# A hybrid attention and RG-LRU layer on one core: modulation quads of four-k groups in pairs, a seventh raw slot, and the rotary tables moved

## The chip, the cores and the metric

The kernel runs on one core of a Trainium2 chip. The metric is the device time of one execution in microseconds (us), a median of runs. The core has five engines that run apart from each other and wait on semaphores: TensorE (PE, with its weight loads shown as PEld), VectorE (DVE), ScalarE (ACT), GpSimd (POOL, which here only issues DMAs) and SyncE (SP, which issues nearly all loads). Line numbers such as L521 are lines of the kernel before, unless the text says "of the changed kernel"; the changed kernel's lines stand up to 8 higher.

## The reference

One layer with x and ctx of 256 tokens by 4096 columns each. What it computes, cut to what matters here:

```python
mod = silu(c) @ w_ada + b_ada                       # shift, scale, gate; also with c_ctx
h_x = rmsnorm(x, norm_w) * (1 + scale_x) + shift_x  # and h_c from ctx
q, k, v, ga, xl, gl = split(h @ w_in)               # 4096 x 9216; for ctx k, v and xl are used
q, k = rope(rmsnorm(q)), rope(rmsnorm(k))           # per head of 128; latent tokens only
att = softmax(q k^T) v                              # keys and values of x and ctx
lru = two scans over short_conv(xl), with gates from block-diagonal weights
mix = concat(rmsnorm(att) * silu(ga), rmsnorm(lru) * silu(gl))
out = x + gate_x * (mix @ w_out)
```

All arithmetic is float32; the large products are made of rounded high and low parts, three matmuls each.

## The kernel before

Every weight comes in pieces of 512 KB into one of six "raw" slots. SP issues these loads in the order of the tasks that use them, and the next one as soon as a slot is free. A planner (`Plan.order`) writes out one fixed order of tasks with its own costs; each engine then runs its part of that order, first come first served.

**Projection stage** (to about 665 us). The 4096 rows of `w_in` are walked in groups of k tiles of 128 rows: groups of 1, 1, 2, 2 and 2 k tiles, then six groups of four ("four-k groups"). In a group each weight piece ("unit") is cast to its high part by ACT (L684) and to its low part by DVE (L688), and PE multiplies it in threes (L785 to L787) into a PSUM bank `pm`; DVE adds the bank to the sums `a` in SBUF (L805), which frees it. There are four `pm` banks. A four-k group has 288 such matmuls.

Beside that, the shift and scale of the next group are made from `w_ada` (`mod_tasks`). A "quad" is four k tiles of `w_ada`, 512 columns wide in a four-k group, and so two loads. The shift half's eight quads run on PE (`on_tensor`, L521): four matmuls of 32 output rows side by side in the array, where the matmuls of L785 use all 128. The scale half runs on DVE (L511, two multiply-adds for each k tile, sums in `xin` and `u`); in the first two four-k groups PE has a part of it too. PE folds DVE's sums in at the end (L534). `RUN` says how many quads one PE task takes: `RUN = {1: 2, 2: 1, 4: 1}` by k tiles in the group, so one quad with two loads in a four-k group. The planner may put any other ready PE task between two such tasks.

**Keys and rotary tables.** `rope_tasks` makes, once for k and once for q, a table of cosines and sines times the norm weights. Its first task clears one column of a `wg` slot on DVE (L465) and then has POOL issue two loads (L466, L467, into `wg` and `u`); its second task multiplies them on DVE (L471, L475) into the tile `rope`. `rotate` (L1002 to L1007) uses `rope` and a scratch tile `td` in SBUF.

**After the projection** come q in four chunks with attention and the 16 LRU blocks beside it (L971 to L973 are the matmuls by weights), then the two gates, and from about 1400 us on the output projection, where `scaled` (L1486, L1487) multiplies by the gate through `td` and adds x. The gate third of `w_ada` is summed on DVE (L906) all along from about 630 us.

Of the kernel before, what the change touches and what calls it, by code (L numbers as in the profile page):

```python
# [14 lines left out]
D = 4096  # L15
# [13 lines left out]
NB = 16  # L29
EPS = 1e-6  # L30
C_Q, C_K, C_V, C_GA, C_XL, C_GL = 0, 2048, 2560, 3072, 5120, 7168
RAW = 6
HL = 3
TP = 2
LAT = dict(P=0.2, A=0.14, D=0.14, S=0.15)
# [9 lines left out]
LRU_CHUNKS = 10.2  # L45
MOD_V = {3: (0, 2), 4: (0, 3), 5: (0, 5), 6: (0, 7)}
MOD_V_REST = (0, 8)
RUN = {1: 2, 2: 1, 4: 1}
SWITCH = 0.40
FIRST = (1, 1, 2, 2, 2)  # L50
MOD_LEAD = 0.34
# [23 lines left out]
def dve(n, k=1):  # L75
    return k * (0.07 + n / 962)
# [142 lines left out]
def kernel(  # L219
# [31 lines left out]
    ctx.enter_context(tc.manual_schedule())  # L251


    SLOTS = dict(h4=(22, 1024), a8=(6, 2048), raw=(RAW, 1024), hi=(HL, 1024), lo=(HL, 1024), tp=(TP, 512), ta=(1, 512), td=(1, 512), wg=(2, 514),
                 xin=(1, 512), u=(1, 512), ga=(1, 512), ab=(2, 16), cf=(1, 16), mx=(3, 2), ss=(5, 16), pm=(4, 512), pe=(2, 512), pt=(1, 512), po=(1, 512))
    ROUNDED = ("h4", "hi", "lo")
    free, owner, keepers = {}, {}, []
# [34 lines left out]
        return slot(cl, [128, 512])  # L292


    plan = Plan({cl: n for cl, (n, _) in SLOTS.items() if cl not in ("raw", "td", "ss", "cf")} | dict(lh=1, ah=3, lg=1), RAW)
    add = plan.add

    def play(tasks):
# [33 lines left out]
    nc.sync.dma_start(cin[:, 1, :], c_ctx.rearrange("(p k) -> p k", p=128))  # L332
    sc32 = [slot("wg", [128, 16 * KT + 2]) for _ in range(2)]
    sc = cp.tile([128, 2, KT], F32, name="sc")
    tnh = slot("td", [128, 2, KT])
    for i in range(2):
        V.memset(sc32[i], 0.0)
    V.memset(epsc, EPS)
# [22 lines left out]
    kwc = parT[:, 1, 112:113]  # L361
    hba, hbx, lam = parT[:, 2, 0:32], parT[:, 2, 32:64], parT[:, 2, 64:96]
    lp = cp.tile([128, 2, 32], F32, name="lp")
    rope = cp.tile([128, 2, 2, 128], F32, name="rope")
    gT = cp.tile([128, KT], F32, name="gT")
    st = cp.tile([128, 4, NG], F32, name="st")
    rs = cp.tile([128, 4], F32, name="rs")
# [87 lines left out]
            a = add(fn, [op], [a], pos + step * i, nb=pos - 2 if i == 0 else None, acq=["tp"] if i == 0 else [], rel=["tp"] if fn is finish else [])  # L455
        return a

    def rope_tasks(w, pos, after):

        d = {}  # L460

        def load():
            d["tab"], d["w"] = slot("u", [128, 2, 2, 128]), slot("wg", [128, 128])

            V.memset(d["w"][:, 0:1], 0.0)  # L465
            Q.dma_start(d["w"], w.to_broadcast([128, 128]))  # L466
            Q.dma_start(d["tab"].rearrange("p t f d -> p (t f d)"), consts[:, 130:642])  # L467

        def mul():
            tab, w_ = d["tab"], d["w"]  # L470
            V.tensor_tensor(out=rope[:, :, 0], in0=tab[:, :, 0], in1=w_.unsqueeze(1).to_broadcast([128, 2, 128]), op=ALU.mult)  # L471
            wv = w_.rearrange("p (a h f) -> p a h f", a=2, h=2)
            for t in range(2):
                for h in range(2):
                    V.tensor_tensor(  # L475
                        out=rope[:, t, 1].rearrange("p (a h f) -> p a h f", a=2, h=2)[:, :, h],
                        in0=tab[:, t, 1].rearrange("p (a h f) -> p a h f", a=2, h=2)[:, :, h], in1=wv[:, :, 1 - h], op=ALU.mult,
                    )
            drop(d["tab"], d["w"])

        a = add(load, [("S", 1.0, 6.0)], after, pos - 12, nb=pos - 14, acq=["u", "wg"])
        return add(mul, [("D", dve(256) + dve(64, 4))], [a], pos, rel=["u", "wg"])


    def mod_tasks(k0, nk, out_, p0, p1, nb, cl, on_v=(0, 0)):
# [394 lines left out]
        else:  # L880
            group_pieces(gi, (0, 1), True)

    k_rope = rope_tasks(k_norm_w, starts[-2] + 16, [p_turned])
    decayed = decay_tasks(starts[-2] + 16, 3.0, p_turned)


# [107 lines left out]
    def rotate(a, t):

        o = slot("td", [128, 4, 128])
        av = a.rearrange("p n (a h f) -> p n a h f", a=2, h=2)
        ov = o.rearrange("p n (a h f) -> p n a h f", a=2, h=2)
        sv = rope[:, t, 1].rearrange("p (a h f) -> p a h f", a=2, h=2)
        for ax in range(2):  # L1000
            for h in range(2):
                V.tensor_tensor(  # L1002
                    out=ov[:, :, ax, h], in0=av[:, :, ax, 1 - h],
                    in1=sv[:, ax, h].unsqueeze(1).to_broadcast([128, 4, 32]), op=ALU.mult,
                )
        V.tensor_tensor(out=a, in0=a, in1=rope[:, t, 0].unsqueeze(1).to_broadcast([128, 4, 128]), op=ALU.mult)
        V.tensor_tensor(out=a, in0=a, in1=o, op=ALU.add)  # L1007
        drop(o)

    ROTATE = dve(128, 4) + dve(512, 2)  # L1010
    res = {}
# [1 line left out]
    def key_tasks(pos):  # L1013
        d = {"ss": slot("ss", [128, 4, 4])}

        def kv(t):
            return accs["k"][:, t].rearrange("p (n d) -> p n d", n=4)

        def mul(t):
            V.tensor_tensor(out=kv(t), in0=kv(t), in1=d["ss"][:, t].unsqueeze(2).to_broadcast([128, 4, 128]), op=ALU.mult)  # L1020

        def turn(t):
            d["pt", t] = bank()
            for n in range(4):
                T.transpose(d["pt", t][:, 128 * n : 128 * n + 128], kv(t)[:, n], ident)

        def put(t):
            if t == 0:
                res["kT"] = a8t([128, 4, 512])
            dst = res["kT"][:, :, 128 * t : 128 * t + 128]  # L1030
            src = d["pt", t].rearrange("p (n k) -> p n k", n=4)
            if t < 2:
                S.copy(dst, src)
            else:
                S.activation(dst, src, AF.Copy, scale=kwc)
            drop(d["pt", t])
            if t == 3:
                drop(accs["k"])

        sq = [add(lambda t=t: sum_squares(kv(t), d["ss"][:, t]), [("A", SUMSQ)], [acc_last["k"]], pos + 2 * t, acq=["ta"], rel=["ta"]) for t in range(4)]  # L1040
        nrm = add(lambda: norm_cols(d["ss"]), [("A", ROOT, "root"), ("D", 0.17)], sq, pos + 8)
        prev, rots = None, []
        for t in range(4):
            p = pos + 10 + 5 * t
            a = add(lambda t=t: mul(t), [("D", dve(512))], [nrm], p)
            if t < 2:
                a = add(lambda t=t: rotate(kv(t), t), [("D", ROTATE)], [a, k_rope], p + 1)
                rots.append(a)
# [8 lines left out]
    def q_head_tasks(j, ps, ends, pos, after):  # L1057
        d = {"ss": slot("ss", [128, 4, 4])}

        def pv(t):  # L1060
            return ps[t].rearrange("p (n d) -> p n d", n=4)

        def mul(t):
            a = d["aa", t] = slot("tp", [128, 4, 128])
            for n in range(4):
                S.activation(a[:, n], pv(t)[:, n], AF.Copy, scale=d["ss"][:, t, n : n + 1])
            drop(ps[t])

# [395 lines left out]
    for j in range(8):  # L1464
# [89 lines left out]
```

## Time and profile before

| | |
|---|---|
| median of 3 runs | 1770.1 us (1766.76 to 1772.22) |
| profiled execution | 1768.89 us, span 1767.1 us, mean granted PE clock 0.995 |
| PE busy | 1712.0 us, 97% of the span |
| DVE busy | 1390.0 us, 79% |
| ACT busy | 854.4 us, 48% |
| raw loads | 800 of 512 KB, 255 GB/s of all DMA over the span |

The span is the time from the first to the last instruction on the core; 1.8 us of the execution lie outside it. [...] A busy engine is not always an engine at its peak: where PE has queued work without a gap, only the distance between starts tells its pace.

### The profile page before, as it was taken

The page shows a single profiled execution, that of the slowest core. Times are in us where ns is not written, and L with a number is a line of the kernel's source. Part 1 is how long each engine was busy: PE and PEld are TensorE (multiplying, and loading weights), DVE is VectorE, ACT ScalarE, POOL GpSimd, SP SyncE. Part 2 cuts the span into 40 slices and gives each one's busy share as a digit, 9 for nine tenths or more (in the row PEclk, how much of TensorE's full clock was granted, in tenths as well). Part 3 has the DMA queues.
Part 4 walks back from the last instruction along what each step waited for, and adds up shares of the span by engine and source line. Part 5 has one row for each costly group of instructions (what it writes and reads, how often), then busy time and mean ns, then how long its engine had stood idle before and what let it go on. Part 6 is the DMA issues. An engine that isn't in the chain of part 4 may idle for free.

```text
span 1767.1 us, 22676 instructions
## 1 busy us (share of the span) xinstructions
PE 1712.0 (97%) x8189; PEld 1310.1 (74%) x8189; DVE 1390.0 (79%) x2001; ACT 854.4 (48%) x1254; POOL 58.3 (3%) x93
## 2 busy tenths in 40 slices
PE   4999999999999998999999999999999999999998
PEld 2455667676776677877777778888788788888887
DVE  2368879798989887566799779989987988686864
ACT  5422232232423233357876867777677543333332
POOL 0000000000000000000000000000000000000000
PEclk9999999999999999999999999999999999999999
DMA  9999988988797874854467548777876799898983
GB/s 326 332 343 328 325 310 258 324 269 309 232 326 259 285 251 135 275 172 132 146 206 231 158 119 274 222 240 216 266 253 191 224 335 335 277 334 270 336 275 113
DMA packets 252976, 451.22 MB, mean 255 GB/s; under 512 B 14848, under 2 KB 56432, under 8 KB 252352
## 3 DMA queue, kind: packets, MB, share of 16 engines
q1 hardware_dynamic: 246624, 428.43, 74.0%
q0 software_dynamic: 6240, 21.35, 3.5%
q8 instruction: 64, 1.05, 0.2%
q14 instruction: 48, 0.39, 0.1%
HBM read 441.33 MB, written 8.39 MB: 254 GB/s over the span
## 4 chain that ended last, share of the span: by engine, by line
PE 66%; DVE 17%; DMA 9%; issue 4%; ACT 4%; SPq 1%; DVEq 0%; POOL 0%; ACTq 0%; POOLq 0%
PE pm L971 13%; PE pm L973 13%; PE pm L972 13%; DMA raw<-in_w_ada_dram 7%; PE pm L785 6%; PE pm L786 6%; PE pm L787 6%; DVE lo L688 5%; DVE u L511 2%; PE po L521 2%; PE pt L521 2%; DVE xin L511 2%; ACT hi L684 2%; DVE ga L906 1%; DVE a L805 1%
## 5 line engine op out<-in xcount | busy, mean ns | idle before, releaser
L684 ACT CAST hi<-raw 128x1024 fp32r<-128x1024 f32 x416 | 435.9, 1049 | 714.9 <-PE pm L973 288.4
L688 DVE TENSOR_TENSOR lo<-raw,hi 128x1024 fp32r<-128x1024 f32 x416 | 505.9, 1220 | 178.2 <-ACT hi L684 176.2
L971 PE MATMUL pm<-hi,h 128*128 128x512 f32 x1280 | 514.4, 402 | 0.0
L972 PE MATMUL pm<-lo,h 128*128 128x512 f32 x1280 | 498.9, 390 | 3.9 <-DVE lo L688 3.8
L973 PE MATMUL pm<-hi,h 128*128 128x512 f32 x1280 | 499.1, 390 | 0.0
L785 PE MATMUL pm<-hi,h 128*128 128x512 f32 x768 | 315.7, 411 | 8.7 <-DVE a L805 7.1
L786 PE MATMUL pm<-lo,h 128*128 128x512 f32 x768 | 302.2, 393 | 0.8 <-DVE lo L688 0.8
L787 PE MATMUL pm<-hi,h 128*128 128x512 f32 x768 | 301.9, 393 | 0.0
L972 PEld LDWEIGHTS pm<-lo,h 128*128 128x128 f32 x1280 | 240.7, 188 | 57.6 <-DVE lo L688 5.6
L971 PEld LDWEIGHTS pm<-hi,h 128*128 128x128 f32 x1280 | 240.5, 188 | 51.7 <-issue 4.8
L973 PEld LDWEIGHTS pm<-hi,h 128*128 128x128 f32 x1280 | 240.2, 188 | 50.9
L785 PEld LDWEIGHTS pm<-hi,h 128*128 128x128 f32 x768 | 145.4, 189 | 97.5 <-issue 47.4
L906 DVE SCALAR_TENSOR_TENSOR ga<-raw,sc,ga 128x512 f32<-128x512 f32 x248 | 185.9, 749 | 7.6 <-DMA raw<-in_w_ada_dram 2.4
L787 PEld LDWEIGHTS pm<-hi,h 128*128 128x128 f32 x768 | 145.6, 190 | 32.1
L786 PEld LDWEIGHTS pm<-lo,h 128*128 128x128 f32 x768 | 145.8, 190 | 27.5 <-DVE lo L688 1.3
L511 DVE SCALAR_TENSOR_TENSOR xin<-raw,sc,xin 128x512 f32<-128x512 f32 (+1 forms) x188 | 135.3, 720 | 31.2 <-DMA raw<-in_w_ada_dram 31.1
L805 DVE TENSOR_TENSOR a<-pm,a 128x512 f32<-128x512 f32 x202 | 132.4, 683 | 32.7 <-PE pm L787 32.3
L511 DVE SCALAR_TENSOR_TENSOR u<-raw,sc,u 128x512 f32<-128x512 f32 (+1 forms) x188 | 135.3, 720 | 0.0
L521 PE MATMUL po<-raw,wg 128*32 128x256 f32 (+2 forms) x560 | 61.7, 474 | 27.2 <-DMA raw<-in_w_ada_dram 27.0
L521 PEld LDWEIGHTS po<-raw,wg 128*32 128x32 f32 x560 | 14.7, 119 | 55.8 <-DMA raw<-in_w_ada_dram 26.1
L645 ACT ACTIVATE ta<-pe,ab 128x256 f32<-128x256 f32 x64 | 36.0, 563 | 38.9 <-PE pe L635 31.3
L521 PE MATMUL pt<-raw,wg 128*32 128x512 f32 (+2 forms) x456 | 48.0, 474 | 4.9 <-DMA raw<-in_w_ada_dram 4.8
(189 smaller groups left out, 1299.8 us busy)
## 6 DMA issues: line engine op xcount, KB each, us to landing
raw<-in_w_ada_dram SPq DMA_DIRECT2D x384, 512.0 KB, 5.6
raw<-in_w_in_dram SPq DMA_DIRECT2D x288, 512.0 KB, 4.7
raw<-in_w_out_dram SPq DMA_DIRECT2D x128, 512.0 KB, 5.0
h<-in_x_dram SPq DMA_DIRECT2D x8, 512.0 KB, 7.7
h<-in_ctx_dram SPq DMA_DIRECT2D x8, 512.0 KB, 10.8
xl_d<-a POOLq DMA_DIRECT2D x4, 1024.0 KB, 6.8
xin<-xl_d POOLq DMA_DIRECT2D x16, 256.0 KB, 4.5
a<-in_x_dram POOLq DMA_DIRECT2D x8, 512.0 KB, 7.0
```

Source lines behind the costliest of these rows:

```text
L511: V.scalar_tensor_tensor(out=a, in0=d["w"][:, i], scalar=s_, in1=a, op0=ALU.mult, op1=ALU.add)
L521: T.matmul(d["ps"][32 * q : 32 * q + 32, :], sc32[half][:, o : o + 32], ws[i // step][:, i % step], start=(part, quad) == first_p, stop=(p ...
L684: S.copy(d["hi"], raw)
L688: V.tensor_tensor(out=d["lo"], in0=d["raw"], in1=d["hi"].bitcast(F32), op=ALU.subtract)
L785: T.matmul(ps[s, t], hi, wh, start=f, stop=False)
L786: T.matmul(ps[s, t], hi, wl, start=False, stop=False)
L787: T.matmul(ps[s, t], lo, wh, start=False, stop=e)
L805: V.tensor_tensor(out=a, in0=ps[s, t], in1=a, op=ALU.add)
L906: V.scalar_tensor_tensor(out=d["acc"], in0=w[:, i], scalar=s_, in1=d["acc"], op0=ALU.mult, op1=ALU.add)
L971: T.matmul(ps[t], hi, wh, start=f, stop=False)
L972: T.matmul(ps[t], hi, wl, start=False, stop=False)
L973: T.matmul(ps[t], lo, wh, start=False, stop=e)
```

## The change

- `RUN[4]` goes from 1 to 2: two neighbouring quads of a four-k group form one PE task with four loads, where both are PE's. PE has 52 quads in these groups. Before they stand in 51 runs on PE (one pair stood together already); now in 28 runs, 24 of them pairs.
- A seventh raw slot (4 KB a partition). Its room comes from `rope` and `td`, which go.
- The table for k lies in a `tp` slot from its multiplication to the last rotation of k; the table for q in `post`'s tile, where the root sums come later. `rotate` has its scratch in a PSUM bank (`pe` for k, `pt` for q). `scaled` multiplies in place in the `pm` bank.
- `rope_tasks` has three tasks: the DVE clearing, the loads, the multiplication. The planner takes the loads to need 9 us instead of 6, and k's multiplication has a later nominal place (+30 instead of +16).

```diff
-RAW = 6
+RAW = 7
-RUN = {1: 2, 2: 1, 4: 1}
+RUN = {1: 2, 2: 1, 4: 2}
...
-    def rope_tasks(w, pos, after):
+    def rope_tasks(z, w, pos, after, place, acq):
         d = {}
+        def open_():
+            d["tab"], d["w"] = slot("u", [128, 2, 2, 128]), slot("wg", [128, 128])
+            V.memset(d["w"][:, 0:1], 0.0)
         def load():
-            d["tab"], d["w"] = slot("u", [128, 2, 2, 128]), slot("wg", [128, 128])
-            V.memset(d["w"][:, 0:1], 0.0)
             Q.dma_start(d["w"], w.to_broadcast([128, 128]))
             Q.dma_start(d["tab"].rearrange("p t f d -> p (t f d)"), consts[:, 130:642])
...
-        a = add(load, [("S", 1.0, 6.0)], after, pos - 12, nb=pos - 14, acq=["u", "wg"])
-        return add(mul, [("D", dve(256) + dve(64, 4))], [a], pos, rel=["u", "wg"])
+        a = add(open_, [("D", 0.06)], after, pos - 16, nb=pos - 18, acq=["u", "wg"])
+        a = add(load, [("S", 1.0, 9.0)], [a], pos - 16)
+        return add(mul, [("D", dve(256) + dve(64, 4))], [a], pos, acq=acq, rel=["u", "wg"])
...
-    k_rope = rope_tasks(k_norm_w, starts[-2] + 16, [p_turned])
+    k_rope = rope_tasks("k", k_norm_w, starts[-2] + 30, [p_turned], lambda: slot("tp", [128, 2, 2, 128]), ["tp"])
...
-    def rotate(a, t):
-        o = slot("td", [128, 4, 128])
+    def rotate(a, t, z, cl):
+        b, r = bank(cl), rope[z]
+        o = b.rearrange("p (n d) -> p n d", n=4)
...
-    q_rope = rope_tasks(q_norm_w, Q0 + 0.8 * CH, rots)
+    add(lambda: drop(rope["k"]), [("D", 0.0)], rots, Q0, rel=["tp"])
+    q_rope = rope_tasks("q", q_norm_w, Q0 + 0.8 * CH, [post["made"]], lambda: post["rope"], [])
...
         def scaled(t, d=d, j=j):
-            o = slot("td", [128, 512])
+            o = d["ps"][t]
```

The order of PE in a four-k group, where the first quads for a later group stand, at about 315 us of the execution before (`raw` are the loads, `wg` the vectors, `pt` the bank of the modulation sums). Before:

```order
L521 MATMUL pt_103<-raw_74,wg_81 32x512 x2
L521 MATMUL pt_103<-raw_75,wg_81 32x512 x2
L785 MATMUL pm_99<-hi_2139,h_1700 128x512
L786 MATMUL pm_99<-lo_2151,h_1700 128x512
L787 MATMUL pm_99<-hi_2139,h_1701 128x512
L785 MATMUL pm_99<-hi_2139,h_1700 128x512
L786 MATMUL pm_99<-lo_2151,h_1700 128x512
L787 MATMUL pm_99<-hi_2139,h_1701 128x512
L521 MATMUL pt_103<-raw_73,wg_81 32x512 x2
L521 MATMUL pt_103<-raw_71,wg_81 32x512 x2
```

The same place on PE in the changed kernel:

```order
L525 MATMUL pt_103<-raw_71,wg_81 32x512 x2
L525 MATMUL pt_103<-raw_73,wg_81 32x512 x2
L525 MATMUL pt_103<-raw_76,wg_81 32x512 x2
L525 MATMUL pt_103<-raw_72,wg_81 32x512 x2
L789 MATMUL pm_99<-hi_2143,h_1706 128x512
L790 MATMUL pm_99<-lo_2145,h_1706 128x512
L791 MATMUL pm_99<-hi_2143,h_1707 128x512
```

The two quads stood with six matmuls of the projection between them and now stand in one run. Behind each pair come 36 to 48 projection matmuls before the next pair, and the loads of one such turn are four for the pair and three or four others.

The order of DVE at the end of the projection stage, around the clearing for k's table (`pm` are the banks that PE waits for, `ga` the sums of the gate). Before:

```order
L688 TENSOR_TENSOR lo_4572<-raw_72,hi_4567 128x1024
L465 MEMSET wg_81 128x1
L471 TENSOR_TENSOR rope<-u_84,wg_81 128x2x128
L475 TENSOR_TENSOR rope<-u_84,wg_81 128x2x32 x4
L906 SCALAR_TENSOR_TENSOR ga_85<-raw_75,sc,ga_85 128x512 x2
L688 TENSOR_TENSOR lo_4612<-raw_71,hi_4610 128x1024
L805 TENSOR_TENSOR a_65<-pm_97,a_65 128x512
L805 TENSOR_TENSOR a_65<-pm_98,a_65 128x512
```

And in the changed kernel:

```order
L692 TENSOR_TENSOR lo_4604<-raw_75,hi_4602 128x1024
L809 TENSOR_TENSOR a_65<-pm_97,a_65 128x512
L809 TENSOR_TENSOR a_65<-pm_98,a_65 128x512
L809 TENSOR_TENSOR a_65<-pm_99,a_65 128x512
L809 TENSOR_TENSOR a_65<-pm_100,a_65 128x512
L692 TENSOR_TENSOR lo_4641<-raw_71,hi_4634 128x1024
L465 MEMSET wg_81 128x1
L910 SCALAR_TENSOR_TENSOR ga_85<-raw_76,sc,ga_85 128x512 x2
```

The multiplication stood right behind the clearing; now the four additions that free `pm` banks stand ahead of the clearing, and the multiplication (L474 of the changed kernel) follows 24 rows behind it, with two low parts, four additions and most of a series of small operations between.

The order of DVE in the first chunk of q, around the clearing for q's table. Before:

```order
L688 TENSOR_TENSOR lo_5143<-raw_75,hi_5141 128x1024
L688 TENSOR_TENSOR lo_5168<-raw_72,hi_5159 128x1024
L465 MEMSET wg_81 128x1
L471 TENSOR_TENSOR rope<-u_84,wg_81 128x2x128
L475 TENSOR_TENSOR rope<-u_84,wg_81 128x2x32 x4
L688 TENSOR_TENSOR lo_5193<-raw_76,hi_5191 128x1024
```

And in the changed kernel:

```order
L692 TENSOR_TENSOR lo_5224<-raw_72,hi_5222 128x1024
L1441 MEMSET a_68 128x128
L465 MEMSET wg_81 128x1
L692 TENSOR_TENSOR lo_5268<-raw_74,hi_5260 128x1024
L692 TENSOR_TENSOR lo_5277<-raw_75,hi_5271 128x1024
L920 TENSOR_TENSOR gT<-pe_101,parT 128x4
L692 TENSOR_TENSOR lo_5295<-raw_76,hi_5286 128x1024
L474 TENSOR_TENSOR a_68<-u_84,wg_81 128x2x128
L478 TENSOR_TENSOR a_68<-u_84,wg_81 128x2x32 x4
```

Three low parts now stand between the clearing and the multiplication.

## Rows read from the trace of the kernel before

**Rows 1.** Windows by stage: busy us of each engine, clock, DMA share.

```profile
core 0: us, PE busy (x) PEld busy (x) DVE busy (x) ACT busy (x) POOL busy (x), PEclk, DMA share, GB/s
0.00:150.00 150.00, 118.36 (x896) 68.94 (x896) 72.12 (x151) 61.85 (x136) 5.83 (x15) 0.98 1.06 336
150.00:650.00 500.00, 493.32 (x2330) 347.68 (x2327) 435.97 (x664) 146.83 (x215) 0.00 (x0) 1.00 0.85 288
```

**Rows 2.** Waits from 157 to 600 us: us in total, times, longest.

```profile
PEld po L521 <- DMA raw<-in_w_ada_dram: 9.5, 12, 1.2
PEld pt L521 <- DMA raw<-in_w_ada_dram: 4.2, 7, 1.2
...
DVE xin L511 <- DMA raw<-in_w_ada_dram: 28.1, 24, 3.3
```

**Rows 3.** Timeline of PE: start us, us, instruction, around quads.

```profile
114.92 0.39 PE L787 MATMUL pm<-hi,h 128*128 128x512 f32 x1
115.23 0.64 PE L521 MATMUL pt<-raw,wg 128*32 128x256 f32 x8
...
116.14 0.39 PE L786 MATMUL pm<-lo,h 128*128 128x512 f32 x1
...
117.06 0.40 PE L787 MATMUL pm<-hi,h 128*128 128x512 f32 x1
117.39 1.07 PE L521 MATMUL pt<-raw,wg 128*32 128x256 f32 x16
...
118.73 0.39 PE L786 MATMUL pm<-lo,h 128*128 128x512 f32 x1
...
419.31 0.39 PE L787 MATMUL pm<-hi,h 128*128 128x512 f32 x1
...
420.67 0.39 PE L787 MATMUL pm<-hi,h 128*128 128x512 f32 x1
420.99 1.06 PE L521 MATMUL po<-raw,wg 128*32 128x512 f32 x8
...
422.32 0.39 PE L786 MATMUL pm<-lo,h 128*128 128x512 f32 x1
```

**Rows 4.** Timeline of PE at the end of the projection stage.

```profile
662.19 0.39 PE L787 MATMUL pm<-hi,h 128*128 128x512 f32 x1
667.28 0.77 PE L785 MATMUL pm<-hi,h 128*128 128x512 f32 x1 [4.70 <-DVE a L805]
...
672.06 0.40 PE L787 MATMUL pm<-hi,h 128*128 128x512 f32 x1
```

**Rows 5.** Timeline of POOL and DVE at the same place.

```profile
656.01 0.54 POOL L467 DMA_DIRECT2D u<-in_shape_consts_dram  x1
...
662.98 0.43 DVE L471 TENSOR_TENSOR rope<-u,wg 128x256 f32<-128x256 f32 x1 [8.11 <-DMA u<-in_shape_consts_dram]
...
666.45 2.48 DVE L805 TENSOR_TENSOR a<-pm,a 128x512 f32<-128x512 f32 x4
```

**Rows 6.** Window behind it, with the granted clock (columns as in the first group).

```profile
668.00:670.00 2.00, 2.00 (x7) 1.52 (x6) 2.00 (x4) 2.00 (x15) 0.00 (x0) 0.50 0.92 344
```

**Rows 7.** Timeline of PE and DVE in the first chunk of q.

```profile
752.92 0.39 PE L971 MATMUL pm<-hi,h 128*128 128x512 f32 x1
755.19 0.50 PE L972 MATMUL pm<-lo,h 128*128 128x512 f32 x1 [1.88 <-DVE lo L688]
...
746.30 0.06 DVE L465 MEMSET wg<- 128x1 f32 x1
753.03 0.42 DVE L471 TENSOR_TENSOR rope<-u,wg 128x256 f32<-128x256 f32 x1 [6.67 <-DMA u<-in_shape_consts_dram]
```

**Rows 8.** Groups by line and form: count, busy us, mean ns of one.

```profile
L805 DVE TENSOR_TENSOR a<-pm,a 128x512 f32<-128x512 f32 x202 | 132.4, 683 | 32.7 <-PE pm L787 32.3
...
L1006 DVE TENSOR_TENSOR tp<-tp,rope 128x512 f32<-128x512 f32 x8 | 5.5, 692 | 0.3
```

**Rows 9.** Window over six quads of one four-k group (columns as in the first).

```profile
404.00:436.00 32.00, 31.47 (x143) 19.76 (x142) 23.86 (x35) 4.38 (x5) 0.00 (x0) 1.00 0.99 354
```

More of the change, by code (lines that the diff above doesn't have):

```diff
@@ L251 @@
     ctx.enter_context(tc.manual_schedule())
-    SLOTS = dict(h4=(22, 1024), a8=(6, 2048), raw=(RAW, 1024), hi=(HL, 1024), lo=(HL, 1024), tp=(TP, 512), ta=(1, 512), td=(1, 512), wg=(2, 514),
+    SLOTS = dict(h4=(22, 1024), a8=(6, 2048), raw=(RAW, 1024), hi=(HL, 1024), lo=(HL, 1024), tp=(TP, 512), ta=(1, 512), wg=(2, 514),
                  xin=(1, 512), u=(1, 512), ga=(1, 512), ab=(2, 16), cf=(1, 16), mx=(3, 2), ss=(5, 16), pm=(4, 512), pe=(2, 512), pt=(1, 512), po=(1, 512))
@@ L292, in bank @@
         return slot(cl, [128, 512])
-    plan = Plan({cl: n for cl, (n, _) in SLOTS.items() if cl not in ("raw", "td", "ss", "cf")} | dict(lh=1, ah=3, lg=1), RAW)
+    plan = Plan({cl: n for cl, (n, _) in SLOTS.items() if cl not in ("raw", "ss", "cf")} | dict(lh=1, ah=3, lg=1), RAW)
     add = plan.add
@@ L334 @@
     sc = cp.tile([128, 2, KT], F32, name="sc")
-    tnh = slot("td", [128, 2, KT])
+    tnh = slot("tp", [128, 2, KT])
     for i in range(2):
@@ L363 @@
     lp = cp.tile([128, 2, 32], F32, name="lp")
-    rope = cp.tile([128, 2, 2, 128], F32, name="rope")
+    rope = {}
     gT = cp.tile([128, KT], F32, name="gT")
@@ L456, in decay_tasks, with load @@
         return a
-    def rope_tasks(w, pos, after):
+    def rope_tasks(z, w, pos, after, place, acq):
         d = {}
-        def load():
+        def open_():
             d["tab"], d["w"] = slot("u", [128, 2, 2, 128]), slot("wg", [128, 128])
             V.memset(d["w"][:, 0:1], 0.0)
+        def load():
             Q.dma_start(d["w"], w.to_broadcast([128, 128]))
@@ L470, in mul @@
             tab, w_ = d["tab"], d["w"]
-            V.tensor_tensor(out=rope[:, :, 0], in0=tab[:, :, 0], in1=w_.unsqueeze(1).to_broadcast([128, 2, 128]), op=ALU.mult)
+            r = rope[z] = place()
+            V.tensor_tensor(out=r[:, :, 0], in0=tab[:, :, 0], in1=w_.unsqueeze(1).to_broadcast([128, 2, 128]), op=ALU.mult)
             wv = w_.rearrange("p (a h f) -> p a h f", a=2, h=2)
@@ L475, in mul @@
                     V.tensor_tensor(
-                        out=rope[:, t, 1].rearrange("p (a h f) -> p a h f", a=2, h=2)[:, :, h],
+                        out=r[:, t, 1].rearrange("p (a h f) -> p a h f", a=2, h=2)[:, :, h],
                         in0=tab[:, t, 1].rearrange("p (a h f) -> p a h f", a=2, h=2)[:, :, h], in1=wv[:, :, 1 - h], op=ALU.mult,
@@ L992 @@
     SUMSQ = 4 * (0.215 + 0.091)
[L994 to L996 removed]
+    def rotate(a, t, z, cl):
+        b, r = bank(cl), rope[z]
+        o = b.rearrange("p (n d) -> p n d", n=4)
         av = a.rearrange("p n (a h f) -> p n a h f", a=2, h=2)
         ov = o.rearrange("p n (a h f) -> p n a h f", a=2, h=2)
[L999 removed]
+        sv = r[:, t, 1].rearrange("p (a h f) -> p a h f", a=2, h=2)
         for ax in range(2):
@@ L1005, in rotate @@
                 )
-        V.tensor_tensor(out=a, in0=a, in1=rope[:, t, 0].unsqueeze(1).to_broadcast([128, 4, 128]), op=ALU.mult)
+        V.tensor_tensor(out=a, in0=a, in1=r[:, t, 0].unsqueeze(1).to_broadcast([128, 4, 128]), op=ALU.mult)
         V.tensor_tensor(out=a, in0=a, in1=o, op=ALU.add)
-        drop(o)
+        drop(b)
     ROTATE = dve(128, 4) + dve(512, 2)
@@ L1046, in key_tasks @@
             if t < 2:
-                a = add(lambda t=t: rotate(kv(t), t), [("D", ROTATE)], [a, k_rope], p + 1)
+                a = add(lambda t=t: rotate(kv(t), t, "k", "pe"), [("D", ROTATE)], [a, k_rope], p + 1, acq=["pe"], rel=["pe"])
                 rots.append(a)
@@ L1085, in q_head_tasks @@
             a = add(lambda t=t: mul(t), [("A", act(128, 4) + 0.2)], [nrm, after], pos + 2 + t, acq=["tp"], rel=["pm"])
-            a = add(lambda t=t: rotate(d["aa", t], t), [("D", ROTATE)], [a, q_rope], pos + 3 + t)
+            a = add(lambda t=t: rotate(d["aa", t], t, "q", "pt"), [("D", ROTATE)], [a, q_rope], pos + 3 + t, acq=["pt"], rel=["pt"])
             a = add(lambda t=t: turn(t), [("P", pe(1024))], [a, prev], pos + 5 + t, acq=["pt"], rel=["tp"])
@@ L1433, in make_post @@
         post.update(ones=t[:, 0:128], r_att=t[:, 128:384], r_lru=t[:, 384:640], sml=t[:, 640:896], sm=t[:, 1024:2048])
+        post["rope"] = t[:, 128:640].rearrange("p (t f d) -> p t f d", t=2, f=2)
         V.memset(post["ones"], 1.0)
@@ L1483, in scaled @@
         def scaled(t, d=d, j=j):
-            o = slot("td", [128, 512])
+            o = d["ps"][t]
             for c in (slice(0, 256), slice(256, 512)) if j == 7 else (slice(0, 512),):
-                V.tensor_tensor(out=o[:, c], in0=d["ps"][t][:, c], in1=d["gb"][:, c], op=ALU.mult)
+                V.tensor_tensor(out=o[:, c], in0=o[:, c], in1=d["gb"][:, c], op=ALU.mult)
                 V.tensor_tensor(out=d["xr"][:, t, c], in0=d["xr"][:, t, c], in1=o[:, c], op=ALU.add)
-            drop(o, d["ps"][t], *([d["gb"]] if t else []))
+            drop(o, *([d["gb"]] if t else []))
         def store(t, d=d, j=j):
```

## The prediction

> **What bounds the kernel now.** I read the windows by stage first: they say which engine has no room, and where. From 150 to 650 us, most of the projection stage, PE is busy 493 of 500 us at the full clock, DVE 436, and the DMA engines 85% [rows 1]. So PE sets the end there, with DVE and DMA close behind; time comes only from less PE time or fewer PE waits. Then I read the waits of that stage, to see what PE waits for: its weight loads for modulation quads wait 13.7 us in all for `w_ada` (9.5 and 4.2), and DVE, for its own part of the modulation, 28.1 us [rows 2]. Last I went through the timeline for gaps of PE over 1.5 us after the start. Two belong to this change: 4.70 us at 662 us, and 1.88 us at 753 us [rows 4, 7]. The rest of the kernel has PE at work almost without a gap, so what is saved in these places reaches the end.
>
> **A quad's price on PE.** Distances between starts tell it, since busy times overlap. Six projection matmuls take 420.67 - 419.31 = 1.36 us, 0.227 each [rows 3]. Around a lone quad 256 wide, the second start behind it comes 116.14 - 114.92 = 1.22 us after the last start before it; without two projection starts (0.45) the quad costs 0.77. Two such quads in one run cost 118.73 - 117.06 - 0.45 = 1.22. So the second adds 0.45, its bare streaming, and 0.77 - 0.45 = 0.32 is what each run pays once, for going from 128-row matmuls to 32-row ones and back. A lone quad 512 wide costs 422.32 - 420.67 - 0.45 = 1.20 [rows 3], close to the 0.32 + 2 x 0.45 = 1.22 that this makes of it.
>
> **The pairs.** 51 runs become 28: 23 x 0.32 = 7.4 us less on PE. That holds where the loads are there in time. What could take it away is at most those 7.4 us; what could come on top is the 13.7 us of load waits, if the seventh slot ended them all. A pair needs four loads on hand instead of two, and has one slot more. Which of the two weighs more I cannot read from any row, so I take the load waits as they are: gain 7.4, bounds 0 and 21.1.
>
> **The table of k.** DVE stands in its own queue for 8.11 us until the table lands, 7.0 us after POOL issued it (656.01 to 662.98). Behind it are the four additions that free the `pm` banks, begun at 666.45 [rows 5]. [...] From 662.19 to 672.06 PE makes 12 starts in 9.87 us; at 0.227 each they would be 2.72, so the stall and its slow clock cost 7.1 us. In the new order the additions stand ahead of the clearing, and the multiplication 24 rows behind it. Among those are two low parts, one for each 24 projection matmuls of the group, so 5.4 us apart, and four additions that wait for PE; I take the distance as 10 us or more, against the 7.0 that the load took. Gain 7.1, bounds 0 and 7.1. What is late next, if the table were late, is the first rotation, which has a further low part and four additions ahead of it.
>
> **The table of q.** The same with 6.67 us for DVE; PE loses 755.19 - 752.92 - 0.23 = 2.0 us [rows 7]. Three low parts now stand between clearing and multiplication. PE uses up a piece in 12 matmuls, 2.72 us, so they cover 5.4 to 8.2 us of the 6.7 from clearing to multiplication [rows 7]. What is left, at most 1.3 us, is less than the 4.7 us of the old wait that PE did not feel. Gain 2.0, bounds 0 and 2.0. POOL issues LRU block 1's loads behind the multiplication, which frees their slot; before, they waited on the same one.
>
> **The start.** With seven slots SP sends one more `w_ada` load ahead of the eight loads of ctx. One load is 0.524 MB, so 1.48 us at the 354 GB/s of a full stretch [rows 9]. Up to 150 us the DMA engines are full (share 1.06) [rows 1], and the same bytes come in another order; I take 0, bounds 0 and 1.5 us lost.
>
> **Scratch in PSUM.** The last addition of 10 rotations and of 18 final scalings now reads PSUM instead of SBUF. DVE takes 683 ns for 512 columns with one input in PSUM and 692 with both in SBUF [rows 8]: nothing to pay. [...] A DVE write to PSUM stands in no row here; its cost lies between 0 and one more pass of 0.7 us for each rotation or scaling, in stretches where DVE is not what ends, so that only the last scaling's 0.7 could reach the end. I take 0, being nearest to the row that reads PSUM. The `td` slot's going removes no wait that I found.
>
> **Sum.** 1768.9 (the profiled execution; the median of the three runs is 1.2 above it, 0.07%) - 7.4 - 7.1 - 2.0 = **1752.4 us**, so 1752.
>
> **Rivals.**
> - *DMA takes the pairs' gain.* From 404 to 436 us, over six quads, DMA moves 354 GB/s at a share of 0.99 [rows 9]. A turn from pair to pair is 36 to 48 projection matmuls and 0.32 + 4 x 0.45 = 2.1 us, so 10.3 to 13.0 us of PE; its seven or eight loads take 10.4 to 11.8 us at that rate. The two are about equal, so PE may only wait where it worked before. For it: 19 of the 51 runs already have waits for loads [rows 2]. Against it: the seventh slot fetches one load more ahead of each dense stretch, 1.5 us for each of six groups. Time 1752.4 + 7.4 = 1760. [...]
> - *The seventh slot ends the load waits.* All 13.7 us go: 1739.
> - *A table is still late*, by its distance in rows being shorter in time than I take it: k's 7.1 us come back, 1760. Against it are the 24 rows.
> - *DVE starves, and the kernel is slower.* A pair's loads stand in a row in SP's queue, so DVE's loads behind them come two loads, 3.0 us, later than behind a lone quad. With 24 pairs that is 71 us of DVE. DVE has 64 us idle from 150 to 650, of which 28 are load waits already [rows 1, 2], so 36 to spare. If nothing else filled the time, 35 us would reach PE, through the fold that waits for DVE's sums and through `pm` banks freed late: 1787. It decides against the change from 18 us on, 3 us in each of six groups. Against it: DVE has low parts and additions to do meanwhile, and the same loads come in the same time.
>
> **How the numbers follow.** Forecast 0.62 (its own range 1746 to 1758: the start's and the scratch's bounds, and a part of the load waits either way); DMA takes the gain 0.15; the waits end 0.12; a table still late 0.06; DVE starves 0.05. The range 1741 to 1763 holds the forecast, the two cases at 1760 and the near half of the one at 1739; left out are the slow case and the far half, about 0.11, and what I have not thought of. A measurement of this kernel can tell about 0.3%, 5.3 us. All cases but the last are faster by more than that of 1770.1 (below 1764.8), the two at 1760 by little: faster 0.90, no change 0.05, slower 0.05.
>
> **What would show it.** Right: 28 runs of 512-wide quads with 0.32 us less for each pair; load waits of these quads near 13.7 us; POOL's table issues ahead of their multiplications by more than they take to land; no PE gap over 1 us for `a` at the end of the projection stage, and a granted clock of 1.00 there. Wrong: load waits inside the pairs that grow by about what the pairs save; DVE waits for `w_ada` well over 28 us with folds that PE waits for; a new gap in the reordered first chunks of q.

## The result and the profile after

The changed kernel takes 1750.7 us (median of 4 runs, 1749.9 to 1752.2) against 1770.5 for the kernel before: a ratio of 0.989, interval 0.9876 to 0.9903, so 1.1% faster. The forecast was 1752.4. The number came out close; that is partly luck: the experiments below show that the largest term of its sum had the wrong cause, and that errors of opposite sign cancelled.

The first view of the changed kernel is the windows by stage, with the columns of [rows 1].

```profile
0.00:150.00 150.00, 118.40 (x900) 69.22 (x901) 72.28 (x152) 62.30 (x136) 5.82 (x15) 0.98 1.07 338
150.00:650.00 500.00, 490.55 (x2365) 356.86 (x2364) 442.02 (x672) 148.57 (x217) 0.00 (x0) 1.00 0.86 295
650.00:700.00 50.00, 50.00 (x221) 41.12 (x220) 39.02 (x84) 17.17 (x45) 2.72 (x5) 1.00 0.52 167
700.00:760.00 60.00, 60.00 (x280) 49.86 (x279) 36.82 (x47) 27.13 (x48) 5.99 (x9) 1.00 0.80 262
```

From 150 to 650 us PE does more matmuls (2365 for 2330) in less busy time: it stands idle more in this stage than before (9.4 us for 6.7), and the loads come a little faster (295 GB/s for 288). From 650 to 760 us PE is busy throughout.

The timeline of PE of the changed kernel around a pair answers to [rows 3].

```profile
171.34 0.39 PE L791 MATMUL pm<-hi,h 128*128 128x512 f32 x1
171.66 1.92 PE L525 MATMUL pt<-raw,wg 128*32 128x512 f32 x16
173.52 0.50 PE L789 MATMUL pm<-hi,h 128*128 128x512 f32 x1
173.86 0.40 PE L790 MATMUL pm<-lo,h 128*128 128x512 f32 x1
```

A pair costs 173.86 - 171.34 - 0.45 = 2.07 us where two lone quads cost 2.40: 0.33 less, as the forecast had it. The waits from 157 to 600 us (us in total, times, longest) answer to [rows 2].

```profile
DVE lo L692 <- ACT hi L688: 21.9, 20, 3.6
DVE xin L515 <- DMA raw<-in_w_ada_dram: 21.7, 10, 3.7
PE pm L789 <- DVE a L809: 6.1, 6, 1.6
PEld pt L525 <- DMA raw<-in_w_ada_dram: 3.1, 7, 1.0
PEld po L525 <- DMA raw<-in_w_ada_dram: 1.7, 4, 0.7
```

The quads' load waits fell from 13.7 to 4.8 us. In their place PE waits for DVE's sums `a`: nine gaps between the projection matmuls numbered 288 and 2016 (counted from 0), five of them 1.3 to 1.6 us. One of them in the timelines of DVE and PE:

```profile
353.94 0.75 DVE L515 SCALAR_TENSOR_TENSOR xin<-raw,sc,xin 128x512 f32<-128x512 f32 x1 [2.12 <-DMA raw<-in_w_ada_dram]
...
361.71 1.88 DVE L809 TENSOR_TENSOR a<-pm,a 128x512 f32<-128x512 f32 x3
...
362.54 0.47 PE L789 MATMUL pm<-hi,h 128*128 128x512 f32 x1 [1.58 <-DVE a L809]
```

DVE stood still for 2.1 us until a `w_ada` load came, then worked without a break for 7.8 us, and reached the additions that free the `pm` banks too late. The rotary tables in the timelines of DVE and POOL answer to [rows 4 to 7]:

```profile
655.53 0.06 DVE L465 MEMSET wg<- 128x1 f32 x1
656.73 0.54 POOL L469 DMA_DIRECT2D u<-in_shape_consts_dram  x1
...
663.33 1.82 DVE L809 TENSOR_TENSOR a<-pm,a 128x512 f32<-128x512 f32 x3
...
668.61 0.42 DVE L474 TENSOR_TENSOR tp<-u,wg 128x256 f32<-128x256 f32 x1
...
738.90 0.06 DVE L465 MEMSET wg<- 128x1 f32 x1
...
747.35 0.42 DVE L474 TENSOR_TENSOR a<-u,wg 128x256 f32<-128x256 f32 x1
```

k's multiplication stands 11.9 us behind its load's issue, and the additions come 5.3 us ahead of it; q's stands 8.5 us behind the clearing. Neither waits. The window behind the old stall has the granted clock, a share of the full one, at 1.00 where it was 0.50:

```profile
668.00:670.00 2.00, 2.00 (x10) 1.65 (x10) 1.83 (x12) 0.16 (x1) 0.00 (x0) 1.00 0.62 234
```

**A ledger of the projection stage.** For each kernel I took the time from the start of projection matmul 288 to that of 2016 (counted from 0) in its profiled execution, and split it. "Work" is 0.2267 us for each step from one projection matmul to the next, and all intervals around other PE work, so the waits for loads inside the quads are in it. "Gaps" are steps from one projection matmul to the next with recorded idle time over 0.05 us; all but one end on DVE's `a` (1.2 us in e5 on ACT's high part). "Slow" is what other such steps take over 0.2267, those at a granted clock of 0.50 among it. "Load waits" is, of the work, what the runs of 512-wide quads take beyond 1.20 (one), 2.06 (two) or 2.92 (three).

| kernel | total | work | gaps | slow | load waits |
|---|---|---|---|---|---|
| before | 495.5 | 482.4 | 2.2 | 10.9 | 13.1 |
| changed | 486.7 | 465.8 | 10.8 | 10.0 | 5.0 |
| e1 tables only | 499.6 | 484.9 | 3.7 | 11.0 | 16.0 |
| e2 slot, singles | 486.9 | 476.3 | 0.0 | 10.6 | 8.5 |
| e3 pairs, six slots | 516.4 | 474.3 | 26.6 | 15.4 | 9.5 |
| e4 old table times | 484.8 | 466.8 | 7.9 | 10.1 | 5.4 |
| e5 runs of three | 542.5 | 483.8 | 38.2 | 20.5 | 10.9 |
| e6 half of DVE's sums | 475.5 | 463.6 | 2.9 | 9.1 | 1.7 |
| e7 DVE seven quads | 491.3 | 479.5 | 1.0 | 10.8 | 13.9 |
| e8 eight slots | 495.8 | 488.0 | 0.0 | 7.8 | 20.5 |
| e9 pairs in two groups | 480.1 | 470.3 | 0.0 | 9.8 | 5.3 |
| e10 scratch in `pe` | 483.2 | 463.5 | 9.8 | 9.9 | 2.5 |
| e11 both edits of e9 and e10 | 482.8 | 472.9 | 0.0 | 9.9 | 8.4 |
| e12 one h slot less | 497.3 | 489.6 | 0.0 | 7.7 | 21.2 |

Executions differ here by 2 to 4 us with the same work: e10 has the changed kernel's order on PE, DVE, ACT and SP up to the end of this stage, and their totals differ by 3.5 us; e11 and e9 differ by 2.7 us.

The planner knows the numbers of slots and the length of a run. So an edit of `RAW`, `RUN`, `MOD_V_REST` or the h slots also gives a new order of tasks: from e1 to e2, for one, the order of PE, DVE and SP's loads changes in many places, and the runs do not part a slot from the order that is planned for it. On PE, ACT and SP, e4, e6 and e10 keep the changed kernel's order through this stage.

### The profile page after: what moved, and what is told of

Read it like the earlier page. It is cut to its first block, busy times and chain, and to the rows that moved or that the text cites. A ratio compares the mean times of both kernels' runs of the same rounds, so it can differ in the third digit from the quotient of the medians.

```text
span 1750.5 us, 22650 instructions
## 1 busy us (share of the span) xinstructions
PE 1696.8 (97%) x8189; PEld 1310.6 (75%) x8189; DVE 1391.3 (79%) x2001; ACT 854.1 (49%) x1254; POOL 58.3 (3%) x93
## 4 chain that ended last, share of the span: by engine, by line
PE 60%; DVE 20%; DMA 9%; issue 5%; ACT 5%; SPq 1%; DVEq 0%; ACTq 0%
PE pm L975 12%; PE pm L977 12%; PE pm L976 12%; DMA raw<-in_w_ada_dram 7%; DVE lo L692 6%; PE pm L789 6%; PE pm L790 5%; PE pm L791 5%; DVE u L515 3%; DVE xin L515 2%; ACT hi L688 2%; DVE ga L910 1%; PE pt L525 1%; DMA raw<-in_w_in_dram 1%; PE po L525 1%
## 5 line engine op out<-in xcount | busy, mean ns | idle before, releaser
L977 PE MATMUL pm<-hi,h 128*128 128x512 f32 x1280 | 499.6, 390 | 0.0
L789 PE MATMUL pm<-hi,h 128*128 128x512 f32 x768 | 313.8, 409 | 10.8 <-DVE a L809 9.4
L525 PE MATMUL po<-raw,wg 128*32 128x256 f32 (+2 forms) x560 | 53.7, 472 | 24.4 <-DMA raw<-in_w_ada_dram 24.4
L525 PE MATMUL pt<-raw,wg 128*32 128x512 f32 (+2 forms) x456 | 44.4, 473 | 4.9 <-DMA raw<-in_w_ada_dram 4.8
## 6 DMA issues: line engine op xcount, KB each, us to landing
h<-in_ctx_dram SPq DMA_DIRECT2D x8, 512.0 KB, 10.1
```

Of the source, the lines that this page charges most:

```text
L525: T.matmul(d["ps"][32 * q : 32 * q + 32, :], sc32[half][:, o : o + 32], ws[i // step][:, i % step], start=(part, quad) == first_p, stop=(p ...
L789: T.matmul(ps[s, t], hi, wh, start=f, stop=False)
L977: T.matmul(ps[t], lo, wh, start=False, stop=e)
```

## The experiments

The theory behind the forecast was that its terms stand apart and add up: runs saved on PE, and two stalls gone. The first four kernels undo the parts one by one, each with the order that the planner makes for it; all ratios are to the kernel before on the same chip.

**e1, only the tables and the scratch.**

```diff
-RAW = 7
-RUN = {1: 2, 2: 1, 4: 2}
+RAW = 6
+RUN = {1: 2, 2: 1, 4: 1}
```

> The changed kernel with six raw slots and single quads again (RAW 6, RUN[4] 1), so that only the tables and the scratch are moved. Theory (the terms stand apart): the gap of 4.7 us at the end of the projection stage and that of 1.9 us in the first chunk of q are gone, everything ahead of 650 us is as before; in the two traces the stretch of the k table was 7.0 us shorter, and that of the q table, after small new waits behind it, 0.2: 1770.5 - 7.2 = 1763. Rival: the k gap closed only because the pairs and the seventh slot had DVE and the loads ahead there; then a gap for `a` comes back at the end of the stage and the time is 1768 to 1770.

Measured 1765.5 us, ratio 0.9965 (0.9955 to 0.9976): 6.2 us faster (4.2 to 8.0). Both gaps are gone, as the windows of e1 show, so the rival falls; the size agrees with 7.2.

```profile
650.00:700.00 50.00, 50.00 (x221) 41.13 (x220) 40.97 (x87) 19.33 (x50) 1.65 (x3) 1.00 0.60 196
700.00:760.00 60.00, 60.00 (x278) 49.85 (x277) 33.68 (x40) 20.24 (x22) 4.89 (x8) 1.00 0.77 255
```

**e2, the slot without pairs** (`RUN` 4: 1, `RAW` 7).

> The changed kernel with single quads (RUN[4] 1), seven slots, tables moved. Quad runs on PE 52, at 1.20 us for one against 2.06 for a pair: 24 x 0.34 = 8.2 us more PE time than the changed kernel. Theory A (each engine's time adds up): slower by 8, so 1759; load waits of the quads near the changed kernel's 4.8 us since the slot is what cut them. Theory B (DVE is the next bound in the projection stage: PE waits for the sums `a` 9.4 us in the changed kernel, 2.6 before): the PE time that singles cost is taken from these waits, which fall to 2 to 3 us: 1752 to 1753.

Measured 1751.8 us, ratio 0.9894 (0.9880 to 0.9907): the changed kernel's time, as near as can be measured. Theory A falls. In the ledger, pairs save 10.5 us of work (465.8 for 476.3, of which 3.5 are load waits) and cost 10.8 us of gaps: one for one, as theory B had it. And the slot with its order, against e1, is worth 0.0071 of 1770.5, 12.6 us; the ledger puts it at 12.7, of which 7.5 are load waits and 3.7 gaps.

**e3, the pairs without the slot** (`RUN` 4: 2, `RAW` 6).

> The changed kernel with six raw slots (RAW 6) and pairs. Theory (the slot is what pays for the pairs' loads): load waits of the 512-wide quads are back at 13.7 us or more, against 4.8 with seven slots: 1759 to 1763. Rival (a pair only needs its four loads once, and the wait for them takes the place of two waits): load waits near 5 to 7 us, time 1751 to 1753, and the slot is worth nothing.

Measured 1782.3 us, ratio 1.0063 (1.0049 to 1.0076): slower than the kernel before, and 17 us slower than e1. Both expectations were too kind, and the first named the wrong wait: load waits inside the quads fell to 9.5, but the gaps for `a` grew to 26.6. Two windows of e3 around the longest gap, with the columns of [rows 1]:

```profile
370.00:377.00 7.00, 2.97 (x12) 2.17 (x12) 7.00 (x11) 0.20 (x1) 0.00 (x0) 1.00 0.76 245
377.00:380.00 3.00, 2.32 (x6) 1.82 (x6) 3.00 (x6) 0.00 (x0) 0.00 (x0) 0.56 0.79 263
```

DVE is busy all the time while PE waits, and behind the gap the clock is granted at 0.56 in the mean; this is in the 4.4 us more under "slow" than in e1. What DVE waited for last ahead of this gap were loads of its own:

```profile
360.99 0.75 DVE L515 SCALAR_TENSOR_TENSOR xin<-raw,sc,xin 128x512 f32<-128x512 f32 x1 [2.21 <-DMA raw<-in_w_ada_dram]
...
365.52 0.75 DVE L515 SCALAR_TENSOR_TENSOR xin<-raw,sc,xin 128x512 f32<-128x512 f32 x1 [1.79 <-DMA raw<-in_w_ada_dram]
...
376.94 0.68 DVE L809 TENSOR_TENSOR a<-pm,a 128x512 f32<-128x512 f32 x1
```

From 365.5 us on it works without a break, and in its fixed order the multiply-adds of these late loads stand ahead of the addition that frees a bank. What ACT waits for from 157 to 600 us shows another part of what the slot does: e1, e2, the changed kernel and e3, in this order, one fence each.

```profile
ACT hi L688 <- DMA raw<-in_w_in_dram: 96.8, 14, 9.8
```

```profile
ACT hi L688 <- DMA raw<-in_w_in_dram: 30.8, 5, 8.4
```

```profile
ACT hi L688 <- DMA raw<-in_w_in_dram: 38.3, 6, 8.5
```

```profile
ACT hi L688 <- DMA raw<-in_w_in_dram: 84.8, 11, 15.2
```

With six slots ACT stands waiting for `w_in` 85 to 97 us, with seven, in singles and pairs, 31 to 38. These waits do not order the gaps, though: e1 has the longest and gaps of only 3.7 us. That a pair's four loads hold four of six slots until PE comes to the pair, so that DVE's loads come late, is the reading that fits; it was not measured by itself.

**e4, the tables at their old times.**

```diff
-        a = add(open_, [("D", 0.06)], after, pos - 16, nb=pos - 18, acq=["u", "wg"])
-        a = add(load, [("S", 1.0, 9.0)], [a], pos - 16)
+        def both():
+            open_()
+            load()
+
+        a = add(both, [("S", 1.0, 6.0)], after, pos - 12, nb=pos - 14, acq=["u", "wg"])
...
-    k_rope = rope_tasks("k", k_norm_w, starts[-2] + 30, ...
+    k_rope = rope_tasks("k", k_norm_w, starts[-2] + 16, ...
```

> The changed kernel with the tables' clearing and loads in one task at their old places (6.0, -12, +16), so that on DVE the multiplication stands right behind the clearing for k and one low part behind it for q; pairs, slot and scratch as changed. Theory (distance from the loads to the multiplication is what closed the gap): the gap of 4 to 5 us for `a` at the end of the projection stage comes back with a granted clock of 0.5 behind it, 7.0 us for k; q's costs 0 to 2: 1758 to 1760. Rival (room in `tp` and PSUM, or the slot, closed it): 1751.

Measured 1756.0 us, ratio 0.9917 (0.9903 to 0.9930), by the ratios 4.8 us more than the changed kernel. The stall is back in the timelines of DVE and PE, and the window behind it has a granted clock of 0.50:

```profile
650.69 0.43 DVE L474 TENSOR_TENSOR tp<-u,wg 128x256 f32<-128x256 f32 x1 [7.40 <-DMA u<-in_shape_consts_dram]
...
654.99 0.76 PE L792 MATMUL pm<-hi,h 128*128 128x512 f32 x1 [3.97 <-DVE a L812]
```

```profile
655.00:656.00 1.00, 1.00 (x3) 0.81 (x4) 1.00 (x3) 1.00 (x7) 0.00 (x0) 0.50 0.99 369
```

From matmul 2016 to 2112 it takes 28.3 us against 21.9, 6.4 more. The end moves by less because its execution was 2.2 us ahead at 2016. The slot and the places in `tp` and PSUM are as changed, so for k the times and the order that they give closed the gap. For q they are not shown to have: in e4 DVE waits 1.84 us for q's table, with one low part between, and PE loses nothing by it.

The next four kernels ask what the gaps for `a` are.

**e5, runs of up to three quads** (`RUN` 4: 3).

> The changed kernel with RUN[4] 3: three quads, six loads, in one PE task where they are neighbours; 21 runs of 512-wide quads instead of 28, seven slots as before. Rival (each run saved is 0.34 us of PE and that is all): 7 x 0.34 = 2.4 us faster than the changed kernel, 1748. Theory (what stands in a row in SP's queue for PE holds the slots, so DVE's loads come late, its additions too, and PE waits for `pm`): six of seven slots are in one run, one is left over, where pairs on six slots left two and lost 17 us to singles: gaps for `a` over 20 us in the projection stage, 1765 to 1785.

Measured 1807.1 us, ratio 1.0209 (1.0193 to 1.0225), 56 us more than the changed kernel: the rival falls, and the theory expected only 14 to 34. The waits from 157 to 600 us:

```profile
ACT hi L688 <- DMA raw<-in_w_in_dram: 83.6, 12, 12.8
DVE lo L692 <- ACT hi L688: 50.5, 24, 7.2
PE pm L789 <- DVE a L809: 25.7, 10, 8.2
```

Two windows show the longest gap, 8.2 us, which ends at 486.6 us:

```profile
478.00:486.00 8.00, 0.42 (x2) 0.00 (x0) 7.46 (x12) 1.05 (x1) 0.00 (x0) 0.68 0.99 358
486.00:490.00 4.00, 3.42 (x8) 2.02 (x10) 3.05 (x5) 0.00 (x0) 0.00 (x0) 0.50 1.04 370
```

Over the stage DVE waits most for high parts that ACT makes late, and 8.8 us for its own `w_ada` loads. Ahead of this gap, though, its last long wait was 3.48 us for `w_ada`, at 455 us; ACT then waited for DVE and PE, not for `w_in`. So which loads begin it differs from gap to gap. In the 4 us from 486 us on the granted clock is 0.50.

**e6, DVE leaves out its sums in `u`.**

```diff
-                    else:
+                    elif v == 0:
                         V.scalar_tensor_tensor(out=a, in0=d["w"][:, i], ...
```

> The changed kernel, but DVE leaves out the multiply-adds into `u` (the scale sums for c_ctx are not computed, all but the first k tile); loads, slots, order and all other work stay. DVE has 188 x 0.66 = 124 us less to do in the projection stage. Theory (PE's gaps for `a`, 10.8 us between the 288th and the 2016th projection matmul, are DVE's work catching up behind late loads): the gaps fall under 3 us, 1740 to 1743. Rival (the gaps are the lateness of the loads alone, which DVE then only waits for): gaps stay at 8 to 11 us, 1749 to 1751.

Measured 1739.6 us, ratio 0.9824 (0.9811 to 0.9838): 11.2 us less than the changed kernel by the medians, 11.7 by the ratios. DVE is busy 106.0 us less (1285.3 for 1391.3; the 124 expected were too many). Gaps 2.9 instead of 10.8, load waits 1.7 instead of 5.0. The rival falls: loads and orders are the same, DVE waits for its loads even longer than the changed kernel's 21.7 us, and yet reaches its additions in time.

```profile
DVE xin L515 <- DMA raw<-in_w_ada_dram: 29.8, 18, 3.5
```

No run gives the single quads the same relief, so e6 shows what the gaps are, and not what pairs would be worth with an idle DVE.

**e7, one quad of four groups from DVE to PE** (`MOD_V_REST` (0, 7)).

> The changed kernel with MOD_V_REST (0, 7): in the last four groups PE takes one more quad and DVE has seven instead of eight. PE: 4 more runs of 1.20 us, 4.8 us. DVE: 4 x 8 multiply-adds of 0.66 us fewer, 21 us. Theory (with pairs and seven slots DVE is the bound that is felt): the gaps for `a`, 10.8 us, go nearly all: 1750.7 + 4.8 - 9 = 1746 to 1748. Rival (the work only moves, the gaps come from the loads' order, which gets no better): 1753 to 1756.

Measured 1753.4 us, ratio 0.9907 (0.9892 to 0.9922); it can't be told from the changed kernel, and lies in the rival's range. The theory's mechanism was half right: the gaps go, 1.0 for 10.8. But the work grows by 13.7 us, of which only 4.8 are the quads: waits for loads take the gaps' place, 13.9 us for 5.0. (This profiled execution took 1757.8 us, 4.4 more than the median, so these waits are the high end.)

```profile
PEld pt L525 <- DMA raw<-in_w_ada_dram: 7.3, 9, 2.7
PEld po L525 <- DMA raw<-in_w_ada_dram: 6.7, 10, 2.3
```

**e8, an eighth slot in place of an h slot, singles, and e12, that h slot missing alone.**

```diff
-RAW = 7
+RAW = 8
-    SLOTS = dict(h4=(22, 1024), ...
+    SLOTS = dict(h4=(21, 1024), ...
```

> The changed kernel with single quads, eight raw slots and one h slot less (21 for 22, which gives the room). Theory (a slot is worth the load waits that it ends): with seven slots and singles 8.5 us of waits stand inside the quads and none for `a`; an eighth slot ends about half of them: 1747 to 1749. Rival (seven are enough, the rest waits on the rate of the transfers; and one h slot less makes the preparation of the next group late): 1751 to 1756.

> Seven slots, single quads, 21 h slots: the kernel with eight slots less its eighth slot, or the one with seven slots and singles less one h slot. If the missing h slot is what made the kernel with eight slots slow (6.0 us of PE waiting for h at 53 us, other small waits for h later): 1764 to 1768, the eighth slot worth nothing or less. If the eighth slot itself did harm by another order of transfers: 1753 to 1756.

e8: 1766.0 us, ratio 0.9971 (0.9962 to 0.9981), 14 us more than e2 and outside both ranges that were expected. e12, the same with seven slots: 1768.2 us, ratio 0.9975 (0.9965 to 0.9985), 14 us more than e2 by the ratios. So the edit of the h slot costs it, and the eighth slot gives nothing that can be measured beside it. But PE's order is not e2's: in e12 ten quads stand between transposes of the next `h` (L639), in five blocks that take 31.8 us, where PE waits for ACT's `h` and for loads. In e2 the same wait for ACT's `h` is 1.7 us. The rows are e12's; about 8 us of the 21.2 under "load waits" are of these ten quads, and not waits for loads alone. How much is the missing slot and how much the new order is open.

```profile
PEld pt L525 <- DMA raw<-in_w_ada_dram: 10.3, 11, 2.4
PEld pe L639 <- ACT h L650: 10.2, 10, 1.5
...
PEld po L525 <- DMA raw<-in_w_ada_dram: 8.0, 13, 1.2
```

**e9, pairs in the first two four-k groups alone.**

```diff
-                    while k + m < KT and m < 4 * RUN[nk] and (k + m) // 4 not in v_quads:
+                    while k + m < KT and m < 4 * (1 if k0 >= 16 else RUN[nk]) and (k + m) // 4 not in v_quads:
```

> The changed kernel with pairs only for the quads of the first two four-k groups, of which DVE has 5 and 7 quads, and single quads for the last four, where DVE has 8; 43 runs instead of 28. Theory (pairs pay where DVE has room, and are given back as waits for `a` where it has none): in the traces the changed kernel is 6.7 us ahead of the one with singles at the 864th projection matmul and 0.7 behind at the 2016th; with its pace up to the one and the singles' behind it: 1751.8 - 6.7 = 1745. Rival (the early gain is only a head start that DVE and the loads take back later, wherever the singles begin): 1750 to 1752.

Measured 1745.4 us, ratio 0.9855 (0.9841 to 0.9868): faster than the changed kernel (by 6.2 us) and than e2 (by 6.9), and what their two traces gave; the rival falls. All nine gaps of the changed kernel stand behind matmul 864, where the quads are for groups in which DVE has 8. e11 against e10, the same edit, gives 3.9 us, so the size is less sure than one comparison says. The ledger has no gaps and load waits of 5.3; the waits from 157 to 600 us:

```profile
PEld po L525 <- DMA raw<-in_w_ada_dram: 3.7, 4, 1.3
PEld pt L525 <- DMA raw<-in_w_ada_dram: 1.0, 2, 0.6
...
DVE lo L692 <- ACT hi L688: 15.5, 17, 2.4
```

**e10, the scratch of q's rotations in `pe`, and e11, that with e9's edit.**

```diff
-            a = add(lambda t=t: rotate(d["aa", t], t, "q", "pt"), ..., acq=["pt"], rel=["pt"])
+            a = add(lambda t=t: rotate(d["aa", t], t, "q", "pe"), ..., acq=["pe"], rel=["pe"])
```

> The changed kernel with the scratch of q's rotations in a `pe` bank (there are two) instead of the only `pt` bank. Theory (the gap of q's table is gone, 1.9 us, but new small waits of PE's transposes into `pt` for the rotations' last addition, 1.5 us in five places and as many more for weights, take it back): these waits go and the time is 1.5 to 2 us shorter, 1749. Rival (the same waits come at the `pe` bank, which the LRU blocks use, or PE had only to wait for the rotation's data): 1750.5 to 1752.

> Pairs in the first two four-k groups and the scratch of q's rotations in `pe`, both edits together. If both theories hold and add up: 1743 to 1744. If only that of the pairs holds: 1745. If neither: 1751.

e10: 1750.5 us, ratio 0.9882 (0.9869 to 0.9896); e11: 1747.3 us, ratio 0.9860 (0.9846 to 0.9873). The edit gives nothing. PE's waits behind q's table, from 699.5 to 1093 us, in the changed kernel and then in e10:

```profile
PE pt L1077 <- DVE tp L1012: 1.5, 5, 0.5
```

```profile
PE pt L1077 <- DVE tp L1012: 2.5, 7, 0.5
```

They stay with a bank to spare, so the only `pt` bank is not their cause.

## Why the prediction was right, by its steps

- **A quad's price on PE: right.** 0.33 us less for a pair.
- **The pairs: the step that failed.** "I take the load waits as they are: gain 7.4". Pairs and slot together gave 0.9965 - 0.9890 of 1770.5, 13.3 us, inside its bounds (0 to 21.1), but by the other part: the slot with its order 12.6, the pairs 0.7, which can't be told from nothing. The load waits did not stay as they were (13.7 to 4.8 us), and what the pairs saved on PE came back as 10.8 us of waits for DVE.
- **The table of k: right.** 7.1 forecast, of the 4.70 us gap of [rows 4] and the clock of 0.50 behind it [rows 6]; 7.0 in the traces (28.9 us from matmul 2016 to 2112 before, 21.9 after), 6.4 in e4's trace.
- **The table of q: the gap went, the gain did not.** 2.0 forecast. The 1.88 us gap is gone, but between matmul 2304 of the projection and number 1152 behind it the changed kernel is only 0.2 us shorter, as new waits of 0.1 to 0.9 us stand in the attention. e10 excludes the scratch bank; their cause stays open.
- **The start: nothing to see.** Matmul 288 starts at 155.5 us against 156.0.
- **Scratch in PSUM: right.** The groups by form, of the changed kernel and then of before, show the writing, which had no row:

```profile
L1007 DVE TENSOR_TENSOR pt<-tp,a 128x128 f32<-128x128 f32 x32 | 9.5, 298 | 1.1 <-ACT h L1083 0.2
...
L1012 DVE TENSOR_TENSOR tp<-tp,pt 128x512 f32<-128x512 f32 x8 | 5.5, 688 | 0.3
```

```profile
L1002 DVE TENSOR_TENSOR td<-tp,rope 128x128 f32<-128x128 f32 x32 | 7.1, 285 | 0.0
```

Writing 128 columns to PSUM took 13 ns more (298 for 285), and reading 512 from it 4 ns less than the 692 of [rows 8].

- **The rivals.** "The seventh slot ends the load waits" was nearer than its 0.12: the waits fell to 4.8 us, and the slot with its order gave 12.6 of its 13.7. "DVE starves" named the wait rightly, PE kept waiting for `pm` (10.8 us of gaps); that a pair's loads ahead of others cause it fits, and was not measured by itself. With seven slots that wait costs what the pairs save, and with six it decides, since e3 is slower than the kernel before. Its sign, DVE's waits for `w_ada` well over 28 us, did not come (21.7): DVE waited no longer in all, but ahead of the gaps shown it waited for a `w_ada` load of its own, 2.12 us in the changed kernel and 1.79 in e3. In e5 high parts that come late from ACT are added to that. Of "19 of the 51 runs" that wait for loads, 19 is the number of waits; they stand in 15 runs. "DMA takes the pairs' gain" gave the right size for the pairs with DVE in DMA's place.
- **The sum.** The tables gave 6.2 of the 9.1, pairs and slot 13.3 of the 7.4, and the sum began 1.6 us below the median before. The tables and the start make the forecast 4.5 us too low, pairs and slot 5.9 too high. That it lies only 1.7 us from the 1750.7 measured is luck.

## What to carry to other kernels

Where one engine is 98% busy and another stands close behind (PE 490.6 and DVE 442.0 of 500 us here), time saved on the first can come back as waits for the second, as it did here one for one; look for the stretch in which that one has room, and make the change there alone (e9). What a longer run of loads for one engine is worth hung here on the slots beside it, and on what DVE had to do: the same edit lost 17 us with six slots, gave nothing with seven, and gained 4 to 7 where DVE had less to do. And where a planner makes the order, one number in it changes more than one thing. A long gap can cost more than its length: 4.70 us of gap cost 7.1 here, since PE worked at a granted clock of 0.50 behind it [rows 6]: the 11 steps from 667.28 to 672.06 us [rows 4] took 4.78 us where 0.227 each make 2.50. The clock was 0.50 behind the gaps of 3.97 us in e4 and 8.17 us in e5 too.

## What the runs showed that I had not expected

- One raw slot of 512 KB, with the order planned for it, is worth 12.6 us in a stage whose DMA share is 0.85 in the mean: ACT's waits for `w_in` fall from 97 to 31 us (e1, e2). An eighth gives nothing beside a missing h slot.
- One h slot of 22 fewer costs 14 us (e12 against e2), with quads and transposes in another order on PE.
- Three quads in a run in place of two make the kernel 56 us slower.
